# Banks of PSUM dealt out anew in two phases of attention heads, and the last output written in two pieces

## The chip, the cores and the metric

The kernel runs on one core of a Trainium2 chip, as one program. The metric is the device time of one execution in microseconds (us), lower is better. TensorE (PE in the profile) multiplies matrices into PSUM, which has eight banks of 128 partitions x 512 float32 values; VectorE (DVE) and ScalarE (ACT) read the banks; SyncE (SP) issues the transfers (DMA) from memory.

## The reference

Two layers of a decoder for 256 tokens of 1024 values. Each layer is attention, then a SwiGLU feed-forward part, both behind an RMS norm whose shift, scale and gate come from a vector c by a matrix (the modulation):

```python
mod = jax.nn.silu(c) @ ada_w[i] + ada_b[i]
sh_a, sc_a, g_a, sh_f, sc_f, g_f = jnp.split(mod[:, None, :], 6, axis=-1)
h = rms_norm(x, attn_norm[i]) * (1.0 + sc_a) + sh_a
y = sparse_mixer(h, ...) if i % 2 == 0 else diff_mixer(h, ...)
x = x + g_a * y
h = rms_norm(x, ffn_norm[i]) * (1.0 + sc_f) + sh_f
x = x + g_f * swiglu(h, ffn_w_gate[i], ffn_w_up[i], ffn_w_down[i])
```

Layer 0 has eight MoBA heads and eight NSA heads and one output projection over both. Layer 1 is differential attention: eight heads, each of two soft-max maps, `a = p0 - lam * p1`, then `a @ v`, a norm of each head's output, and the output projection.

## The kernel before

Every large matrix arrives in row tiles of 128 x 1024 (512 KB) in a ring of five buffers, `raw`. ScalarE rounds a tile to `hi` (L188), VectorE takes the rest as `lo` (L189), and three matmuls (hi, lo, hi) make a product of nearly full precision (`mm3`). Activations lie transposed as pairs of such parts in `bigT`. All matmuls outside transposes go through `mm` (L114 to L116), so the profile shows them as L116.

`banks(acc, sc, tr, ot)` says which banks the next phase takes for what: `SC` for scores, `TR` for transposes, `OT` for the heads' outputs. `bank(*SC)` deals them out in turn. In the second phase of heads of both layers `SC` is 0, 1, 2, `TR` is 4, 5, `OT` is 6, 7, and bank 3 is handed to the modulation. In the phase ahead of it in both layers `TR` is 6, 7, and transposes that began there still use them.

A head pair goes through these steps. `softmax_maps` (L878) takes a bank for each of two maps, multiplies q by k (TensorE), then for each half of the tokens VectorE adds the mask and finds the maximum (L892), and ScalarE takes the exponential (L894) into tiles `s`, of which there are four. `transpose_map` (L908) transposes a map by three matmuls with the identity (L911) into a bank of `TR`, and ScalarE copies it to `pT` (L913). `av` (L916) multiplies `pT` with the values into a bank of `OT`, in two steps by key block. In layer 0 `split` then makes `bigT` of the bank. In layer 1 `diff_heads` (L1227) combines two maps into one ahead of the transposes (L1253 to L1257), copies the output to `od`, and `finish` (L1230) norms it, multiplies it (L1236), transposes it (L1238) into a bank of `TR` and splits it.

Beside the heads runs `ada_pe` (L323), for columns j = 4 and then 3 of the modulation: VectorE clears a bank (L326), then eight raw tiles come (L329), and each takes four matmuls of one output row, `raw,cs` in the profile. ScalarE copies the sums out (L318), two transposes (L320) turn them into columns, and VectorE adds the bias (L355).

`weave` calls the generators of heads and of modulation in turn, and `late` chains them. That is the order in which the code records; the order on each engine is set by the framework's scheduler from dependencies and its own estimates. Each engine, and SP's queue of transfers, runs its list strictly in order. Behind the heads comes `out_proj` (L533) into banks 0 to 3, with eight tiles of weights through the same `raw` ring, then `res_norm` (L442), whose transposes are L407.

At the end of layer 1's feed-forward part (`ffn`, L674 to L680) the last six blocks of the down projection are kept back: for each half of the tokens (t) and of the columns (f) 18 matmuls of 512 columns close one bank, and `res_norm` multiplies that bank by the gate (L452), adds it to `xs` (L455) and sends the 256 KB out (L457).

## Time and profile before

| | us |
|---|---|
| median of three runs (lowest, highest) | 751.43 (750.35, 752.98) |
| the profiled execution | 752.87 |
| its span | 750.8 |
| PE busy | 706.4 (94%) |
| DVE busy | 504.5 (67%) |
| ACT busy | 414.6 (55%) |
| share of the 16 DMA engines taken by the queue of transfers | 61.9% |

Busy time of PE is modelled and overlaps, so 94% is not TensorE at its peak. The chain of work that ended last says what kept the end back; the timeline lists the instructions in order of time, with the idle time ahead of one in brackets and what ended it; windows give busy time, granted clock of TensorE (PEclk, 1.00 is 2.4 GHz and 0.50 is 1.2 GHz) and DMA share of a stretch. In the timeline one matmul leaves one or two records, so the four matmuls on one raw tile show as x8. `kTm,qTm` and `kTn,qT` are scores, `ident,s` transposes of maps, `pT,...` and `pcT,vblk` products with values, `hi,bigT` and `lo,bigT` out_proj.

### The profile page before, as it was taken

The numbers are of one execution on the slowest core, as the hardware profiler recorded it, in microseconds if no ns is written. First come the engines' busy times: TensorE is split into PE (matmuls) and PEld (weight loads), VectorE is DVE, ScalarE is ACT, GpSimd is POOL, SyncE is SP. The second block draws the span as 40 slices with busy tenths as digits, with TensorE's granted clock in tenths as the row PEclk, the third lists the DMA queues.
The fourth block names the chain that finished last, engine by engine and source line by source line (L and its number), as shares of the span: only waits on it lengthen the run. The fifth ranks groups of instructions, "written<-read, shape, count | busy, mean of one in ns | idle before, by whom it ended". The sixth has DMA issues, their size and how long they took to land.

```text
span 750.8 us, 10789 instructions
## 1 busy us (share of the span) xinstructions
PE 706.4 (94%) x3822; PEld 540.6 (72%) x3822; DVE 504.5 (67%) x1078; ACT 414.6 (55%) x813; POOL 40.8 (5%) x131
## 2 busy tenths in 40 slices
PE   5799899799989999999999999997989999999997
PEld 1368567445668878888887787763667888888885
DVE  3558565666587789788855765846777796655632
ACT  3465734688466456545544665566557465555530
POOL 5004102000000000000000021110000000000000
PEclk9999999799999999999999999899899999999999
DMA  9938286067538899998851564008937886566501
GB/s 321 379 127 313 76 296 246 1 234 276 192 91 274 284 339 338 314 305 299 280 193 60 196 223 141 29 18 304 345 113 257 309 292 212 172 196 192 179 20 57
DMA packets 86525, 159.41 MB, mean 212 GB/s; under 512 B 6199, under 2 KB 48316, under 8 KB 86472
## 3 DMA queue, kind: packets, MB, share of 16 engines
q1 hardware_dynamic: 85992, 158.72, 61.9%
q8 instruction: 30, 0.49, 0.3%
q14 instruction: 23, 0.19, 0.1%
q0 software_dynamic: 480, 0.01, 0.0%
HBM read 157.66 MB, written 1.05 MB: 211 GB/s over the span
## 4 chain that ended last, share of the span: by engine, by line
PE 77%; DMA 8%; DVE 6%; ACT 5%; issue 3%; SPq 1%; DVEq 0%; ACTq 0%
PE bank L116 73%; PE bank L911 2%; DMA araw<-in_ada_w_dram 2%; DMA bias<-in_ada_w_dram 2%; DMA raw<-in_ada_w_dram 1%; DMA raw<-in_sp_w_in_dram 1%; DVE lo L189 1%; DMA xs<-in_x_dram 1%; DMA raw<-in_ffn_w_gate_dram 1%; PE bank L711 1%; ACT hi L188 1%; DVE ada_acc L282 1%; PE bank L407 1%; ACT bigT L188 1%; DVE bigT L189 1%
## 5 line engine op out<-in xcount | busy, mean ns | idle before, releaser
L189 DVE TENSOR_TENSOR lo<-raw,hi 128x1024 fp32r<-128x1024 f32 x131 | 156.6, 1205 | 54.2 <-ACT hi L188 53.6
L188 ACT ACTIVATE hi<-raw 128x1024 fp32r<-128x1024 f32 x131 | 135.2, 1043 | 69.9 <-PE bank L116 43.3
L116 PE MATMUL bank<-hi,bigT 128*128 128x512 f32 (+1 forms) x472 | 154.0, 397 | 5.2 <-ACT bigT L188 4.4
L116 PE MATMUL bank<-bigT,hi 128*128 128x512 f32 (+1 forms) x400 | 130.8, 379 | 0.0
L116 PEld LDWEIGHTS bank<-hi,bigT 128*128 128x128 f32 x472 | 89.2, 192 | 26.0 <-ACT bigT L188 5.3
L116 PE MATMUL bank<-bigT,lo 128*128 128x256 f32 x368 | 98.5, 281 | 0.0
L116 PE MATMUL bank<-lo,bigT 128*128 128x512 f32 (+1 forms) x236 | 93.8, 398 | 0.5 <-DVE lo L189 0.4
L116 PEld LDWEIGHTS bank<-bigT,hi 128*128 128x128 f32 x400 | 71.7, 189 | 12.8 <-DVE lo L189 0.4
L282 DVE SCALAR_TENSOR_TENSOR ada_acc<-araw,cs,ada_acc 128x1024 f32<-128x1024 f32 x46 | 58.8, 1278 | 20.1 <-DMA araw<-in_ada_w_dram 20.1
L116 PEld LDWEIGHTS bank<-bigT,lo 128*128 128x128 f32 x368 | 69.5, 189 | 3.8 <-issue 0.2
L116 PEld LDWEIGHTS bank<-lo,bigT 128*128 128x128 f32 x236 | 45.3, 192 | 13.4 <-DVE lo L189 3.9
L892 DVE CUSTOM_DVE_ANT_0 s<-bank,maskc,nrs 128x128 f32<-128x128 f32 (+1 forms) x80 | 29.9, 412 | 32.0 <-PE bank L116 15.5
L620 ACT ACTIVATE w2k<-bank 128x256 f32<-128x256 f32 x64 | 23.9, 379 | 34.0 <-PE bank L116 34.0
L894 ACT ACTIVATE s<-s,mx 128x128 f32<-128x128 f32 (+1 forms) x80 | 35.7, 448 | 10.5 <-DVE mx L892 10.3
L621 DVE TENSOR_TENSOR w2k<-bank,w2k 128x256 f32<-128x256 f32 x64 | 26.5, 417 | 10.0 <-ACT w2k L620 10.0
L116 PE MATMUL bank<-bigT,nkv 128*128 128x256 f32 (+1 forms) x176 | 31.5, 322 | 0.0
L189 DVE TENSOR_TENSOR tok<-raw,tok 128x1024 fp32r<-128x1024 f32 x19 | 23.2, 1220 | 9.2 <-ACT tok L188 9.1
L188 ACT ACTIVATE nkv<-raw 128x1024 fp32r<-128x1024 f32 x19 | 20.1, 1057 | 16.1 <-PE bank L116 8.1
L189 DVE TENSOR_TENSOR nkv<-raw,nkv 128x1024 fp32r<-128x1024 f32 x19 | 23.2, 1222 | 7.7 <-ACT nkv L188 7.6
L188 ACT ACTIVATE tok<-raw 128x1024 fp32r<-128x1024 f32 x19 | 20.1, 1058 | 13.7 <-PE bank L116 9.5
L116 PEld LDWEIGHTS bank<-bigT,nkv 128*128 128x128 f32 x176 | 25.5, 188 | 2.8
L394 ACT ACTIVATE xn<-xs 128x512 f32<-128x512 f32 x16 | 10.1, 630 | 30.1 <-DVE xs L455 24.3
(342 smaller groups left out, 1257.7 us busy)
## 6 DMA issues: line engine op xcount, KB each, us to landing
araw<-in_ada_w_dram SPq DMA_DIRECT2D x50, 512.0 KB, 5.3
raw<-in_ffn_w_gate_dram SPq DMA_DIRECT2D x44, 512.0 KB, 5.1
raw<-in_ffn_w_up_dram SPq DMA_DIRECT2D x44, 512.0 KB, 4.9
raw<-in_ffn_w_down_dram SPq DMA_DIRECT2D x44, 512.0 KB, 5.2
raw<-in_ada_w_dram SPq DMA_DIRECT2D x32, 512.0 KB, 5.1
raw<-in_diff_w_in_dram SPq DMA_DIRECT2D x24, 512.0 KB, 4.5
raw<-in_sp_w_in_dram SPq DMA_DIRECT2D x20, 512.0 KB, 6.0
raw<-in_nsa_cmp_w_dram SPq DMA_DIRECT2D x8, 512.0 KB, 5.1
```

The lines of the kernel that those rows point to most:

```text
L116: ins = T.matmul(o, lhsT=lhsT, rhs=rhs, start=start, stop=stop).ins
L188: i1 = A.activation(out=hi, in_=src, func=AF.Copy)
L189: i2 = V.tensor_tensor(out=lo, in0=src, in1=hi.bitcast(F32), op=ALU.subtract)
L282: ins = V.scalar_tensor_tensor(out=acc, in0=raw, scalar=cs[:, k:k + 1], in1=acc, op0=ALU.mult, op1=ALU.add)
L394: return A.activation(out=junk[:, fs], in_=xs[:, t, fs], func=AF.Square, accum_out=ss[:, f:f + 1])
L407: q = T.transpose(out=b[:, k * P:(k + 1) * P], in_=xn[:, f * 512 + k * P:f * 512 + (k + 1) * P], identity=ident)
L620: A.activation(out=s[:, f * S:(f + 1) * S], in_=bs[f][:, S:512], func=AF.Copy)
L621: V.tensor_tensor(out=s[:, f * S:(f + 1) * S], in0=bs[f][:, 0:S], in1=s[:, f * S:(f + 1) * S], op=ALU.add)
L711: T.transpose(out=b[:, k * P:(k + 1) * P], in_=src[:, k * P:(k + 1) * P], identity=ident)
L892: V.tensor_tensor_reduce(out=s[:, o:o + n], in0=b[:, o:o + n], in1=maskc[:, S - n:S], scale=nr(t), scalar=3e38, op0=ALU.add, op1=ALU.min, ...
L894: A.activation(out=s[:, o:o + n], in_=s[:, o:o + n], func=AF.Exp, scale=-1.0, bias=mx[:, t:t + 1], accum_out=sm[:, t:t + 1])
L911: T.transpose(out=b[:, k * P:(k + 1) * P], in_=s[:, k * P:(k + 1) * P], identity=ident)
```

## The change

In both phases `SC` gets a fourth bank, 3; `OT` keeps bank 6 alone; the modulation's bank is 7 instead of 3. At the end, for the last half of tokens and of columns, the 18 matmuls become 2 x 18 of 256 columns each, and multiplication, addition and transfer go in two pieces of 256 columns. Both pieces lie in the same bank, and only the last of the 36 matmuls has `stop` set. Lines behind the additions move by 7 (from L451 on) and by 17 (from L678 on).

```diff
--- before.py
+++ after.py
@@ -448,6 +448,13 @@
         marks = []
         for f in range(2):
             fs = slice(f * 512, (f + 1) * 512)
+            if last and t and f:
+                for e in (512, 768):
+                    es = slice(e, e + 256)
+                    V.tensor_tensor(out=xn[:, es], in0=bs[t][f][:, e - 512:e - 256], in1=g[:, es], op=ALU.mult)
+                    V.tensor_tensor(out=xs[:, t, es], in0=xs[:, t, es], in1=xn[:, es], op=ALU.add)
+                    dma(out[0, t * P:(t + 1) * P, es], xs[:, t, es])
+                return
             y = xn[:, fs]
             m = V.tensor_tensor(out=y, in0=bs[t][f], in1=g[:, fs], op=ALU.mult)
             if t and not last:
@@ -674,6 +681,16 @@
             keep = chain[:]
             chain[:] = tail
             for fs in ((0,), (1,)):
+                if nxt[2] is None and t and fs[0]:
+                    for e in (0, 256):
+                        for k in ks:
+                            ah, al = acts[k // 2]
+                            cc = slice((k % 2) * S + t * P, (k % 2) * S + (t + 1) * P)
+                            hi, lo = us[k - ks[0]]
+                            c = slice(512 + e, 768 + e)
+                            mm3(BS[t][1][:, e:e + 256], ah[:, cc], al[:, cc], hi[:, 0, c], lo[:, 0, c], False,
+                                e > 0 and k == ks[-1])
+                    continue
                 for k in ks:
                     down_mm(t, k, us[k - ks[0]], fs)
             tail[:] = chain
@@ -1297,12 +1314,12 @@
     nh = nsa_heads(*on)
     weave((late(np_, first(nh, 6)), 22), (moba_proj(hts), 20), (ada(0, 2, pin=True), 9))
     hts = new_hts()
-    banks([], [0, 1, 2], [4, 5], [6, 7])
+    banks([], [0, 1, 2, 3], [4, 5], [6])
     settle()
     plan((), R5)
     ordr = [4, 5, 6, 7, 0, 1, 2, 3]
     pre = [row_unit(sp_w_out[0], ordr[m]) for m in range(1)]
-    weave((late(nh, moba_heads(*om)), 22), (late(*[ada_pe(0, j, bank_tiles[3]) for j in (4, 3)]), 14))
+    weave((late(nh, moba_heads(*om)), 22), (late(*[ada_pe(0, j, bank_tiles[7]) for j in (4, 3)]), 14))
     plan(R5[1:] + (('qT', 'kTn'), 'tok4'), R5)
     banks([], [], FGU, [])
     drain(out_proj([om, on], sp_w_out[0], ordr, rows[(0, 2)], (0, 3, hts), pre))
@@ -1323,8 +1340,8 @@
     ob_ = pair()
     hts = new_hts()
     plan(R5 + (('qT', 'kTn'), 'tok4'), R5)
-    banks([], [0, 1, 2], [4, 5], [6, 7])
-    weave((diff_heads(1, st, *ob_), 12), (late(*[ada_pe(1, j, bank_tiles[3]) for j in (4, 3)]), 14))
+    banks([], [0, 1, 2, 3], [4, 5], [6])
+    weave((diff_heads(1, st, *ob_), 12), (late(*[ada_pe(1, j, bank_tiles[7]) for j in (4, 3)]), 14))
     banks([], [], FGU, [])
     drain(out_proj([oa, ob_], diff_w_out[0], range(8), rows[(1, 2)], (1, 3, hts)))
     plan(*FFN_PLAN)
```

How this moves instructions is shown at three places. In the names `bank_67` is bank 0, `bank_70` bank 3, `bank_71` to `bank_74` banks 4 to 7.

Layer 0, TensorE, near the end of the heads. Before (`pT,vm` are products with values, `ident,s` transposes of maps, `hi`, `lo`, `qT`, `kTn`, `tok` out_proj's weights):

```order
L116 MATMUL bank_74<-pT_1794,vm_784 64x256 [waits Activation_49]
L116 MATMUL bank_74<-pT_1786,vm_784 64x128
L116 MATMUL bank_74<-pT_1794,vm_784 64x128
L911 MATMUL bank_72<-ident,s_1814 128x128 x3
L320 MATMUL bank_71<-ident,w2k_1844 128x128 [waits Activation_49]
L320 MATMUL bank_71<-ident,w2k_1844 128x128
L116 MATMUL bank_73<-pT_1834,vm_784 64x256
L116 MATMUL bank_67<-tok_1979,bigT_771 128x512 [waits Activation_49]
L116 MATMUL bank_67<-tok_1980,bigT_771 128x512 [waits DVE_49]
L116 MATMUL bank_67<-tok_1979,bigT_771 128x512 [waits DVE_49]
L116 MATMUL bank_73<-pT_1842,vm_784 64x256 [waits Activation_49]
L116 MATMUL bank_73<-pT_1834,vm_784 64x128
```

After, at the same maps:

```order
L928 MATMUL bank_71<-ident,s_1812 128x128 [waits Activation_49]
L928 MATMUL bank_71<-ident,s_1812 128x128 [waits DVE_49]
L928 MATMUL bank_71<-ident,s_1812 128x128
L928 MATMUL bank_72<-ident,s_1814 128x128 [waits Activation_49]
L928 MATMUL bank_72<-ident,s_1814 128x128 [waits DVE_49]
L928 MATMUL bank_72<-ident,s_1814 128x128
L116 MATMUL bank_67<-qT_1973,bigT_771 128x512 [waits Activation_49]
L116 MATMUL bank_67<-kTn_1974,bigT_771 128x512
L116 MATMUL bank_73<-pT_1786,vm_784 64x256 [waits DVE_49]
L116 MATMUL bank_73<-pT_1794,vm_784 64x256
L116 MATMUL bank_73<-pT_1786,vm_784 64x128
L116 MATMUL bank_73<-pT_1794,vm_784 64x128
```

The three transposes of one map and of its partner stand together, and the four matmuls with the values of one pair stand in one run instead of two.

Layer 1, VectorE, the clearing of the modulation's bank. Before (`L892` are the score reductions of a map, `s` and `mx` their results):

```order
L892 ISA s_4761,mx_4771<-bank_68,maskc,nrs_4223 128x256
L892 ISA mx_4771 128x1
L892 ISA s_4763,mx_4774<-bank_69,maskc,nrs_4223 128x256
L892 ISA mx_4774 128x1
L892 ISA s_4811,mx_4815<-bank_67,maskc,nrs_4223 128x128 [waits PE_49,Activation_49]
L892 ISA mx_4815 128x1
L326 MEMSET bank_70 128x256 [waits Activation_49]
L892 ISA s_4813,mx_4818<-bank_68,maskc,nrs_4223 128x128 [waits PE_49]
L892 ISA mx_4818 128x1
L892 ISA s_4811,mx_4821<-bank_67,maskc,nrs_4223 128x256 [waits DVE_49]
```

After (`L909` are the same reductions, `L1274` the combination of two maps, `L1253` the multiplication of od):

```order
L1253 SCALAR_TENSOR_TENSOR od_4422<-od_4422,rs_y_4700,gout 128x128 [waits DVE_49]
L1253 SCALAR_TENSOR_TENSOR od_4422<-od_4422,rs_y_4700,gout 128x128 x3
L1274 SCALAR_TENSOR_TENSOR s_4863<-s_4865,sm_4866,s_4863 128x256
L909 ISA s_4961,mx_4966<-bank_70,maskc,nrs_4223 128x128 [waits PE_49]
L909 ISA mx_4966 128x1
L909 ISA s_4959,mx_4969<-bank_69,maskc,nrs_4223 128x256
L909 ISA mx_4969 128x1
L909 ISA s_4961,mx_4972<-bank_70,maskc,nrs_4223 128x256
L909 ISA mx_4972 128x1
L189 TENSOR_TENSOR bigT_4218<-bank_74,bigT_4218 128x256 [waits Activation_49]
L189 TENSOR_TENSOR bigT_4218<-bank_73,bigT_4218 128x256 [waits Activation_49]
L326 MEMSET bank_74 128x256 [waits DVE_49]
```

The clearing moved from behind the fifth reduction of the phase to behind all sixteen, behind od's multiplications and the two splits of the banks 7 and 6.

The same place on TensorE, where the first matmuls on raw tiles wait for it. Before:

```order
L116 MATMUL bank_69<-kTm_4220,qTm_4219 128x128 [waits DVE_49]
L116 MATMUL bank_69<-kTm_4220,qTm_4219 128x256
L116 MATMUL bank_70<-raw_4749,cs 1x256 [waits DMAHW4_49,DVE_49]
L116 MATMUL bank_70<-raw_4749,cs 1x256 x3
L116 MATMUL bank_70<-raw_4777,cs 1x256 [waits DMAHW5_49]
L116 MATMUL bank_70<-raw_4777,cs 1x256 x3
```

After (`L1255` are od's transposes, `nkv,pT` products with values):

```order
L928 MATMUL bank_71<-ident,s_4863 128x128 [waits DVE_49,Activation_49]
L1255 MATMUL bank_74<-ident,od_4422 128x128 [waits DVE_49] x2
L1255 MATMUL bank_73<-ident,od_4422 128x128 [waits DVE_49] x2
L928 MATMUL bank_71<-ident,s_4863 128x128 [waits DVE_49]
L928 MATMUL bank_71<-ident,s_4863 128x128
L116 MATMUL bank_73<-nkv_4221,pT_4791 128x128 [waits DVE_49]
L116 MATMUL bank_73<-nkv_4221,pT_4791 128x128
L116 MATMUL bank_73<-nkv_4222,pT_4791 128x128
L116 MATMUL bank_74<-raw_4749,cs 1x256 [waits DMAHW4_49,DVE_49]
L116 MATMUL bank_74<-raw_4749,cs 1x256 x3
```

The matmuls on raw tiles moved from behind the scores of the third map to behind the transposes of three maps, od's transposes and a product with values.

The tail on VectorE. Before:

```order
L455 TENSOR_TENSOR xs<-xs,xn_6821 128x512 [waits DVE_49]
L452 TENSOR_TENSOR xn_6865<-bank_69,mod_6743 128x512 [waits PE_49]
L455 TENSOR_TENSOR xs<-xs,xn_6865 128x512 [waits DVE_49]
L452 TENSOR_TENSOR xn_6865<-bank_70,mod_6743 128x512 [waits PE_49]
L455 TENSOR_TENSOR xs<-xs,xn_6865 128x512 [waits DVE_49]
```

After:

```order
L459 TENSOR_TENSOR xn_6883<-bank_69,mod_6743 128x512 [waits PE_49]
L462 TENSOR_TENSOR xs<-xs,xn_6883 128x512 [waits DVE_49]
L454 TENSOR_TENSOR xn_6883<-bank_70,mod_6743 128x256 [waits PE_49]
L454 TENSOR_TENSOR xn_6883<-bank_70,mod_6743 128x256
L455 TENSOR_TENSOR xs<-xs,xn_6883 128x256 [waits DVE_49] x2
```

One multiplication and one addition became two of each; the second multiplication waits for nothing of its own.

## Rows read from the trace of the kernel before

**Rows 1.** The page's chain that ended last: share of the span by engine
```profile
PE 77%; DMA 8%; DVE 6%; ACT 5%; issue 3%; SPq 1%; DVEq 0%; ACTq 0%
```

**Rows 2.** Windows: us, then PE, PEld, DVE, ACT, POOL busy (count); PEclk; DMA share; GB/s
```profile
180.00:190.00 10.00, 10.00 (x53) 6.89 (x47) 8.75 (x20) 10.00 (x24) 0.00 (x0) 1.00 0.82 290
...
512.00:516.00 4.00, 3.35 (x23) 2.50 (x21) 2.88 (x13) 3.79 (x19) 0.00 (x0) 1.00 1.02 409
...
524.00:528.00 4.00, 2.21 (x19) 0.71 (x19) 2.48 (x13) 0.43 (x2) 0.00 (x0) 0.70 1.01 389
528.00:532.00 4.00, 3.39 (x10) 2.37 (x9) 3.08 (x4) 3.82 (x6) 0.00 (x0) 0.50 1.01 396
532.00:536.00 4.00, 4.00 (x19) 3.23 (x18) 3.35 (x5) 2.77 (x4) 0.00 (x0) 0.95 0.91 315
```

**Rows 3.** Timeline, layer 0, PE: start us, busy us, engine, line, out<-in, records
```profile
146.74 0.88 PE L116 MATMUL bank<-pT,nkv 128*64 128x256 f32 x8
147.55 0.55 PE L911 MATMUL bank<-ident,s 128*128 128x128 f32 x3
...
157.05 0.65 PE L116 MATMUL bank<-pT,nkv 128*64 128x256 f32 x2
157.63 0.55 PE L911 MATMUL bank<-ident,s 128*128 128x128 f32 x3
158.11 0.61 PE L116 MATMUL bank<-raw,cs 128*1 128x256 f32 x8
158.65 0.86 PE L116 MATMUL bank<-pT,nkv 128*64 128x256 f32 x6
159.45 0.55 PE L911 MATMUL bank<-ident,s 128*128 128x128 f32 x3
...
164.63 0.93 PE L116 MATMUL bank<-kTm,qTm 64*128 64x128 f32 x8
165.49 0.65 PE L116 MATMUL bank<-pT,nkv 128*64 128x256 f32 x2
...
166.55 1.04 PE L116 MATMUL bank<-raw,cs 128*1 128x256 f32 x16
167.52 0.86 PE L116 MATMUL bank<-pT,nkv 128*64 128x256 f32 x6
```

**Rows 4.** Timeline, layer 0, PE: first run, the one wait, and the stretch's end
```profile
149.46 0.65 PE L116 MATMUL bank<-pT,nkv 128*64 128x256 f32 x4
...
198.19 0.86 PE L116 MATMUL bank<-pT,vm 128*64 128x256 f32 x6 [0.59 <-ACT pT L913]
...
210.84 1.04 PE L407 MATMUL bank<-ident,xn 128*128 128x128 f32 x8
```

**Rows 5.** Timeline, layer 1, PE: first modulation, first refilled raw tile, start of out_proj
```profile
503.81 2.34 PE L116 MATMUL bank<-raw,cs 128*1 128x256 f32 x40
...
508.18 0.61 PE L116 MATMUL bank<-raw,cs 128*1 128x256 f32 x8 [0.68 <-DMA raw<-in_ada_w_dram]
...
528.95 2.07 PE L116 MATMUL bank<-hi,bigT 128*128 128x512 f32 x4 [0.61 <-ACT hi L188]
```

**Rows 6.** Timeline, layer 1, DVE: the memset of the modulation's bank, the second bigT split
```profile
503.49 0.27 DVE L326 MEMSET bank<- 128x256 f32 x1
...
513.39 0.42 DVE L189 TENSOR_TENSOR bigT<-bank,bigT 128x256 fp32r<-128x256 f32 x1
```

**Rows 7.** Chain of waits, layer 1: start us, us, what ended it
```profile
519.77 6.65 DMA raw<-in_ada_w_dram
...
527.95 0.95 ACT hi L188
```

**Rows 8.** Timeline, tail: matmuls of 256 columns on PE, the last multiplication on DVE
```profile
716.05 1.58 PE L116 MATMUL bank<-bigT,tok 128*128 128x256 f32 x12
717.47 1.59 PE L116 MATMUL bank<-bigT,nkv 128*128 128x256 f32 x12
...
746.09 0.69 DVE L452 TENSOR_TENSOR xn<-bank,mod 128x512 f32<-128x512 f32 x1 [2.77 <-PE bank L116]
```

## The prediction

> **What bounds the kernel now.** I read the chain of work that ended last first: 77% of the span is TensorE at work, 8% waits for DMA [rows 1]. So time can come only from TensorE being kept from its work, or from work that TensorE does badly. The three stretches that the change touches differ in this. In the second phase of heads of layer 0, with its out_proj (149.46 to 210.84 us [rows 4]), the windows show TensorE busy all the time, and no wait but one of 0.59 us [rows 2, 4]. What is lost there is seen only in the timeline: inside a run of matmuls of one kind starts follow at 0.05 to 0.11 us, but from the last start of a run to the first of another kind 0.2 to 0.3 us pass, and 64 such runs stand between 149.46 and the transposes of the next norm at 210.84. I read a run's price from its first start to the next run's: 0.58 us for a product with the values of two records, 0.80 for one of six, 0.81 for one of eight, 0.48 for three transposes, 0.54 for the modulation's matmuls on one raw tile, 0.97 on two, 0.86 for a pair's scores [rows 3]. In layer 1 the same phase is bound elsewhere: TensorE is busy 2.21 of 4 us in 524:528, while the DMA engines are full [rows 2], and the longest links of the chain are waits for modulation weights [rows 7]. In the tail TensorE ends, then VectorE multiplies and adds 512 columns, then the last DMA goes out [rows 8].
>
> **Layer 0.** The work stays, its order changes: with a fourth bank the scores of a pair stand further ahead of their use, transposes come six together instead of three, and the two halves of a product with the values, which had transposes or modulation between them, stand in one run in five places. I priced every run of both orders with the prices above. Products with the values: 17 runs become 12; five times 0.58 + 0.80 becomes one of 0.81, so 13.06 goes to 10.23 us, -2.83. Modulation: 12 runs to 9, and each run saved is worth 2 x 0.54 - 0.97 = 0.11 or, where it had been cut inside a tile, up to 0.5; together -0.74. Transposes of maps: 15 runs to 12, -0.34. Scores: 6 to 8 runs, since four are now cut to a half or quarter, +0.89. The few runs of out_proj and of the modulation's own transposes: -0.28. Sum -3.30, from 60.1 to 56.8 us of priced work, against 61.4 in the trace [rows 4]. What is above the price is waits, 0.59 us of it in [rows 4]; with maps ready earlier that one should go. But new ones can come: four banks of scores are also out_proj's accumulators, so its first matmuls into the banks read last now stand behind VectorE's reading of them, and the last heads' output has its split behind a single bank. I bound these by nothing and by the 0.59 of [rows 4] at two places, 1.2. The one bank for heads' outputs adds no other wait: the next product follows over a microsecond behind the split. So layer 0 gives between -4.1 and -2.1; I take the middle, **-3.1**. No later stage holds this back: 210.84 and everything after it is released by events, not by a clock.
>
> **Layer 1.** Here the same rule of banks moves the modulation. Its bank 7 was a transposing bank of the phase ahead, and od's transposes of the first pair still go there. So the memset of bank 7 on VectorE, at 503.49 in the trace, now stands behind the soft-max of all four maps, od's multiplications and the two bigT splits; before it stood five scores reductions into the phase. All that stands ahead of it was done in the trace when the second bigT split ended, at 513.39 + 0.42 [rows 6]. Less its own memset, and with the four transposes in one group, I put the new memset at 513.3 to 513.6 and the first matmul on a raw tile at 513.9, between 513.0 and 515.0, against 503.81 [rows 5]. What queues behind that wait on TensorE: products with values of the later maps, and with each of the 16 raw tiles the release of one of five raw buffers, thus SP's issue of the next transfer, the last eight of which are the weights of out_proj. The price runs through DMA: from the first modulation matmul to the landing of the first refilled tile 508.18 - 503.81 = 4.37 us [rows 5]; then 512 KB at 409 GB/s is 1.28 us each [rows 2]. The first out_proj tile is the twelfth: 4.37 + 11 x 1.28 = 18.45; the hi split takes 0.95 [rows 7], with the step to TensorE 1.05. So out_proj starts 19.5 us behind the first modulation matmul, at 533.4 instead of 528.95 [rows 5]: +4.5. The delay of 10.1 us is not all paid, because before, the stream stood still between the two modulations (the chain's 6.65 us [rows 7]), which the new order doesn't. Against this stands a price of the clock: out_proj begins at half clock, 0.50 in 528:532 and 0.95 in 532:536 [rows 2], behind a stretch in which TensorE waited; the excess is about half of 3.5 us, 1.7. By this estimate TensorE idles earlier and longer, from 505 to 514, and meets out_proj with sparse modulation matmuls, so the excess is the same 1.7 or, with one more such stretch, 3.4; I take it as 0.5 more, nearer to the row: **+5.0**, between +3.0 (first matmul at 513.0, no half clock left) and +7.3 (515.0 and one more such 1.7).
>
> **Tail.** The 18 matmuls of 512 columns become 36 of 256. Twelve of 256 take 717.47 - 716.05 = 1.42 us in the trace [rows 8], 0.118 each, so 36 take 4.26 against 18 x 0.233 = 4.19, +0.07. The two pieces are in one bank and only the last matmul signals, so VectorE begins where it began: four operations of 256 columns, 0.42 us with 0.34 between starts (the bigT split in [rows 6]), against two of 0.69 [rows 8]: 1.44 to 1.68 against 1.40. The last DMA is half as large. Net between -0.4 and +0.4, taken **+0.1**. If the first piece were free to start while the second's 2.1 us of matmuls run, it would save 0.7; the order has no such wait.
>
> **A rule weighed.** In layer 0 the trace shows no wait for a bank, 10.00 of 10 us busy with ScalarE as full in 180:190 [rows 2]; what I count as gain is only the change of kind. The Trainium skill (TensorE: Matmul & The Clock Gate, section HAM oscillation) tells of a kernel in which double-buffered PSUM gave no further gain once TensorE was kept fed; by it the fourth bank is worth nothing here, layer 0 is 0 and the sum +5.1. The rows give -3.1, because the order changes with the banks.
>
> **The rivals.**
> - *The late modulation is hidden* (faster). If VectorE reaches the memset early, or out_proj's first weights don't bind, layer 1 costs 0 to 2.5. It decides at 528.95 - 19.5 = 509.4: a first modulation matmul before that costs nothing. For it: the pause in the stream goes. Against it: the memset's place on VectorE, 10 us of work further back. Own time 752.87 - 3.1 + 0.1 to + 2.6, so 748.4 to 750.9.
> - *The fourth bank buys nothing* (slower): ScalarE, full in 180:190 [rows 2], sets the pace of layer 0, and the drains that go are replaced by waits for its pT copies. It decides where ScalarE's idle time in that phase ends. Layer 0 is 0, the sum +5.1: 756.5. This is also what the page's sentence would give.
> - *Half clock through out_proj* (slower): TensorE's long idle stretch in layer 1 keeps the granted clock at 0.50 for a second stretch as long as that in [rows 2]: +1.7, 755.1. It decides where the clock rises, before or after the first raw tile of out_proj is used up. The Trainium skill (same page, Why this matters for your kernels) warns of idle gaps between bursts; the 0.70 in 524:528 agrees.
> - *The tail overlaps after all*: -0.7, inside the forecast's range.
>
> **How the numbers follow.** Sum -3.1 + 5.0 + 0.1 = +2.0. The profiled execution took 752.87 us (span 750.8), so it would take 754.9; it is 1.44 above the median of the three runs, 751.43, so against that 753.4. Its own range is 751.5 to 755.3. What can be told from no change is 0.3%, 2.25 us: 749.2 to 753.7. Chances: forecast 0.48 (same 0.30, slower 0.18); modulation hidden 0.19 (faster 0.11, same 0.08); fourth bank buys nothing 0.13 (slower); half clock 0.10 (slower); several small things otherwise 0.10 (same 0.06, slower 0.04). Together faster 0.11, same 0.44, slower 0.45. The range leaves out the lower half of the hidden case and the top of the slow ones: 749.2 to 756.8.
>
> **What would show it.** Layer 0: the transposes of the next norm at 207.7 instead of 210.84, 54 runs, TensorE still without gaps. Layer 1, all 3.1 earlier: first modulation matmul near 510.8, behind a memset that ends then; DMA nearly idle until 511.5, then full without a pause; out_proj at 530.3, 19.5 us behind the first modulation matmul instead of 25.1; half clock at its start. Tail: four VectorE rows of 256 columns in a row behind the last matmul. I am wrong if the memset runs before 509 in the old count, if layer 0 ends less than 2 us earlier, or if out_proj in layer 1 starts at once at full clock.

## The result, and the profile after

The changed kernel is slower: 758.65 us median (757.61 to 758.85, four runs), against 750.89 (748.90 to 752.98) for the kernel before on the same chip; the ratio on record is 1.0121, 95% interval 1.0094 to 1.0148 (the two medians alone give 1.0103). The prediction had 753.4 and a range up to 756.8, so it had the direction and not the size: 2.0 us were forecast, 7.8 came. The profiled execution took 758.58 us (span 756.9) against 752.87 (750.8).

The page's chain that ended last now reads (share of the span by engine):

```profile
PE 69%; DMA 12%; DVE 8%; ACT 6%; issue 2%; SPq 1%; DVEq 0%; ACTq 0%
```

Against [rows 1] TensorE's share fell from 77% to 69%, and those of DMA, VectorE and ScalarE rose from 8, 6 and 5%: TensorE is kept from its work for longer. To see where, follow TensorE's timeline of after (start us, busy us, engine, line, out<-in, records, idle before and its releaser) through the landmarks of the prediction: the start of layer 0's phase, the end of its out_proj, the first scores of layer 1's two phases of heads, the first modulation matmul, out_proj, the next norm:

```profile
125.97 1.97 PE L116 MATMUL bank<-kcT,qT 128*128 128x32 f32 x16
...
205.72 1.03 PE L407 MATMUL bank<-ident,xn 128*128 128x128 f32 x8
...
459.71 0.93 PE L116 MATMUL bank<-kTn,qT 64*128 64x128 f32 x8
...
498.13 0.93 PE L116 MATMUL bank<-kTm,qTm 64*128 64x128 f32 x8
...
513.36 3.59 PE L116 MATMUL bank<-raw,cs 128*1 128x256 f32 x32
...
535.76 1.20 PE L116 MATMUL bank<-hi,bigT 128*128 128x512 f32 x4 [0.80 <-ACT hi L188]
...
558.89 1.03 PE L407 MATMUL bank<-ident,xn 128*128 128x128 f32 x8
```

The same landmarks of before, where they are not in [rows 4, 5]:

```profile
128.30 1.97 PE L116 MATMUL bank<-kcT,qT 128*128 128x32 f32 x16
...
465.14 0.93 PE L116 MATMUL bank<-kTn,qT 64*128 64x128 f32 x8
...
500.29 0.93 PE L116 MATMUL bank<-kTm,qTm 64*128 64x128 f32 x8
...
553.15 1.03 PE L407 MATMUL bank<-ident,xn 128*128 128x128 f32 x8
```

Subtracting neighbours gives the account of the two profiled executions, in us (the tail's row goes from the last norm to VectorE's last multiplication, 746.09 in [rows 8] and 752.31 after):

| stretch | before | after | difference | predicted |
|---|---|---|---|---|
| start to layer 0's phase | 128.30 | 125.97 | -2.33 | 0 |
| layer 0: phase and out_proj | 82.54 | 79.75 | -2.79 | -3.1 |
| to layer 1's heads | 254.30 | 253.99 | -0.31 | 0 |
| layer 1, first phase of heads | 35.15 | 38.42 | **+3.27** | 0 |
| second phase, to the first modulation matmul | 3.52 | 15.23 | +11.71 | +10.1 |
| from there to out_proj | 25.14 | 22.40 | -2.74 | -5.6 |
| out_proj | 24.20 | 23.13 | -1.07 | +0.5 |
| rest, to the last multiplication | 192.94 | 193.42 | +0.48 | +0.1 |

The first row is chance: the fourteen profiled executions come in two kinds that part within the first 42 us, by about 4 us, and the one of before was of the late kind (this landmark stands at 124.2 to 126.6 eleven times, at 128.3 to 128.7 three times). So below, single terms are judged by stretches of the traces, whole kernels by their ratio.

The expensive rows are in layer 1. VectorE, second phase (the same columns):

```profile
508.46 1.13 DVE L1253 SCALAR_TENSOR_TENSOR od<-od,rs_y,gout 128x128 f32<-128x128 f32 x4
...
510.98 0.75 DVE L189 TENSOR_TENSOR bigT<-bank,bigT 128x256 fp32r<-128x256 f32 x2
511.78 0.27 DVE L326 MEMSET bank<- 128x256 f32 x1
```

TensorE beside it, ahead of the first modulation matmul at 513.36, and the waits of the chain (start us, us, what) that follow up to out_proj:

```profile
511.79 1.65 PE L116 MATMUL bank<-nkv,pT 128*128 128x128 f32 x6 [1.05 <-DVE bigT L189]
```

```profile
519.20 7.83 DMA raw<-in_ada_w_dram
...
527.75 5.62 DMA raw<-in_ada_w_dram
```

Windows of after (us, then PE, PEld, DVE, ACT, POOL busy; PEclk; DMA share; GB/s):

```profile
508.00:512.00 4.00, 2.37 (x9) 1.42 (x9) 3.95 (x18) 3.08 (x11) 0.00 (x0) 0.50 0.00 0
512.00:516.00 4.00, 4.00 (x34) 2.09 (x38) 1.25 (x6) 1.48 (x8) 0.00 (x0) 0.50 0.13 24
516.00:520.00 4.00, 4.00 (x40) 2.17 (x32) 0.50 (x3) 1.20 (x6) 0.00 (x0) 0.80 0.94 320
520.00:524.00 4.00, 2.11 (x27) 0.52 (x26) 1.96 (x12) 1.58 (x7) 0.00 (x0) 1.00 1.01 380
...
532.00:536.00 4.00, 1.90 (x19) 0.65 (x20) 1.18 (x4) 1.97 (x5) 0.00 (x0) 1.00 0.99 355
```

VectorE is full while TensorE stands at half clock and no DMA moves at all; then, from 520 on, the DMA engines are full, at less than the 409 GB/s of [rows 2]. This is the predicted picture, only larger. What the prediction does not have is the stretch before it. TensorE in layer 1's first phase, where no line was changed; before:

```profile
471.95 1.60 PE L911 MATMUL bank<-ident,s 128*128 128x128 f32 x6
473.43 1.65 PE L116 MATMUL bank<-vm,pT 128*128 128x128 f32 x6
475.01 1.66 PE L116 MATMUL bank<-kTn,qT 64*128 64x128 f32 x8
476.60 1.50 PE L116 MATMUL bank<-vm,pT 128*128 128x128 f32 x6
```

After:

```profile
467.00 1.08 PE L928 MATMUL bank<-ident,s 128*128 128x128 f32 x3 [0.31 <-DVE s L1274]
468.31 2.05 PE L116 MATMUL bank<-kTn,qT 64*128 64x128 f32 x8 [0.22 <-DVE mx L909]
470.29 1.65 PE L116 MATMUL bank<-vm,pT 128*128 128x128 f32 x6
473.59 1.65 PE L116 MATMUL bank<-vm,pT 128*128 128x128 f32 x6 [1.66 <-ACT od L1284]
```

The scores of the fourth pair of maps (the last `kTn,qT` rows) and the first product with values (`vm,pT`) have changed places. ScalarE then has the fourth pair's exponentials (L911) to do ahead of copying that product's output to `od` (L1284), and the second product waits 1.66 us for the copy. ScalarE in after:

```profile
472.45 0.49 ACT L911 ACTIVATE s<-s,mx 128x256 f32<-128x256 f32 x1
...
472.94 0.60 ACT L1284 ACTIVATE od<-bank,sm 128x128 f32<-128x128 f32 x2
```

### The profile page after: what moved, and what is told of

Same layout as the page of the kernel before. It is cut to its first block, busy times and chain, and to the rows that moved or that the text cites. A ratio compares the mean times of both kernels' runs of the same rounds, so it can differ in the third digit from the quotient of the medians.

```text
span 756.9 us, 10831 instructions
## 1 busy us (share of the span) xinstructions
PE 704.2 (93%) x3840; PEld 542.8 (72%) x3840; DVE 505.9 (67%) x1080; ACT 415.2 (55%) x813; POOL 40.5 (5%) x131
## 3 DMA queue, kind: packets, MB, share of 16 engines
HBM read 157.66 MB, written 1.05 MB: 210 GB/s over the span
## 4 chain that ended last, share of the span: by engine, by line
PE 69%; DMA 12%; DVE 8%; ACT 6%; issue 2%; SPq 1%; DVEq 0%; ACTq 0%
PE bank L116 66%; DMA araw<-in_ada_w_dram 3%; DMA raw<-in_ada_w_dram 3%; DMA raw<-in_sp_w_in_dram 2%; DMA bias<-in_ada_w_dram 1%; DMA raw<-in_ffn_w_gate_dram 1%; ACT s L911 1%; PE bank L928 1%; DVE lo L189 1%; DMA xs<-in_x_dram 1%; DVE s L909 1%; ACT hi L188 1%; DMA raw<-in_diff_w_out_dram 1%; DVE bigT L189 1%; PE bank L728 1%
## 5 line engine op out<-in xcount | busy, mean ns | idle before, releaser
L116 PE MATMUL bank<-hi,bigT 128*128 128x512 f32 (+1 forms) x472 | 151.7, 392 | 7.1 <-ACT bigT L188 4.4
L909 DVE CUSTOM_DVE_ANT_0 s<-bank,maskc,nrs 128x128 f32<-128x128 f32 (+1 forms) x80 | 29.9, 413 | 34.0 <-PE bank L116 16.2
L911 ACT ACTIVATE s<-s,mx 128x128 f32<-128x128 f32 (+1 forms) x80 | 35.6, 448 | 11.1 <-DVE mx L909 10.4
L189 DVE TENSOR_TENSOR tok<-raw,tok 128x1024 fp32r<-128x1024 f32 x19 | 23.2, 1221 | 10.1 <-ACT tok L188 10.1
L394 ACT ACTIVATE xn<-xs 128x512 f32<-128x512 f32 x16 | 10.1, 629 | 33.2 <-DVE xs L462 26.9
L188 ACT ACTIVATE tok<-raw 128x1024 fp32r<-128x1024 f32 x19 | 20.1, 1057 | 13.6 <-PE bank L116 10.4
```

The costliest lines, as they stand in the source:

```text
L116: ins = T.matmul(o, lhsT=lhsT, rhs=rhs, start=start, stop=stop).ins
L188: i1 = A.activation(out=hi, in_=src, func=AF.Copy)
L189: i2 = V.tensor_tensor(out=lo, in0=src, in1=hi.bitcast(F32), op=ALU.subtract)
L394: return A.activation(out=junk[:, fs], in_=xs[:, t, fs], func=AF.Square, accum_out=ss[:, f:f + 1])
L909: V.tensor_tensor_reduce(out=s[:, o:o + n], in0=b[:, o:o + n], in1=maskc[:, S - n:S], scale=nr(t), scalar=3e38, op0=ALU.add, op1=ALU.min, ...
L911: A.activation(out=s[:, o:o + n], in_=s[:, o:o + n], func=AF.Exp, scale=-1.0, bias=mx[:, t:t + 1], accum_out=sm[:, t:t + 1])
```

## Experiments

Ratios are against the kernel before on the same chip, with 95% intervals; they are the ratios on record, not the quotients of the two medians. Of an edit only the lines that matter are shown, and `...` stands for lines left out; a line put in without the one that it replaces replaces the same line as in l0 or l1.

### The three parts alone

**l0**, the banks of layer 0 alone:

```
-    banks([], [0, 1, 2], [4, 5], [6, 7])
+    banks([], [0, 1, 2, 3], [4, 5], [6])
...
-    weave((late(nh, moba_heads(*om)), 22), (late(*[ada_pe(0, j, bank_tiles[3]) for j in (4, 3)]), 14))
+    weave((late(nh, moba_heads(*om)), 22), (late(*[ada_pe(0, j, bank_tiles[7]) for j in (4, 3)]), 14))
```

> Kernel before with the new banks in layer 0 alone. Theory A (two effects that cancel): the second phase of heads of layer 0 with its out_proj ends about 2.8 us earlier counted from 130 us, but layer 1's first phase of heads, which has no changed line, loses about 2.9 us between 465 and 478 us as in the changed kernel, because the banks 0, 1, 2 are dealt out in turn by one counter for layer 0's scores and layer 1's accumulators, and it now stands at another bank. Time within 1 us of before. Rival B (the loss at 470 us came from layer 1's own new banks, or is chance): no loss there, 2.8 us faster, 748.1.

750.89 against 749.48 us; 1.0030 [1.0003, 1.0057]. In the trace the stretch from the first matmul on `kcT` to the next norm takes 78.97 us instead of 82.54, but layer 1's first phase takes 39.51 instead of 35.15: layer 0's gain (part of the 3.57 us is the clock's, as the point on layer 0 below works out) is lost 250 us further on, in code of which no line differs. The loss is larger than expected, and the kernel is a little slower than before, not within 1 us of it.

**l1**, the same edit in layer 1 alone:

```
-    banks([], [0, 1, 2], [4, 5], [6, 7])
-    weave((diff_heads(1, st, *ob_), 12), (late(*[ada_pe(1, j, bank_tiles[3]) for j in (4, 3)]), 14))
+    banks([], [0, 1, 2, 3], [4, 5], [6])
+    weave((diff_heads(1, st, *ob_), 12), (late(*[ada_pe(1, j, bank_tiles[7]) for j in (4, 3)]), 14))
```

> Kernel before with the new banks in layer 1 alone. Theory A: first matmul on a modulation tile 15 us behind the phase's first scores instead of 3.5, out_proj 37.6 us behind them instead of 28.7, out_proj itself 1.1 us shorter since the clock is up again, no loss at 465 to 478: 8.3 us slower, about 759. Rival B: the loss at 470 us shows here: 11 us slower, about 762. Rival C (most of the changed kernel's loss was chance of DMA): 5 us slower, 756.

759.4 us; 1.0140 [1.0098, 1.0181]. The first phase keeps its 35.14 us; the second reaches out_proj after 38.66 instead of 28.66 us. So layer 1's banks alone cost about 10 us, twice what the prediction put down for them.

**tail**, the output in two pieces alone (the first two pieces of the change's diff).

> Kernel before with the tail in two pieces alone. Theory A: VectorE starts behind the last of 36 matmuls, four operations one behind another, nothing overlaps; the last transfer is half as large: -0.3 to +0.3 us, no difference that can be measured. Rival D (the pieces overlap or the smaller transfer pays): 0.7 us faster.

747.55 us; 0.9980 [0.9954, 1.0007], no difference that can be told. The rows of after show why: the second multiplication follows the first at once, and both stand behind TensorE's last matmul, as the one multiplication does in [rows 8]:

```profile
752.31 0.76 DVE L454 TENSOR_TENSOR xn<-bank,mod 128x256 f32<-128x256 f32 x2 [2.79 <-PE bank L116]
752.98 0.75 DVE L455 TENSOR_TENSOR xs<-xs,xn 128x256 f32<-128x256 f32 x2
```

### Which of the two bank edits delays layer 1's second phase

**l1_ada7**: in layer 1 the modulation in bank 7 and one bank for outputs, but three banks for scores.

```
+    banks([], [0, 1, 2], [4, 5], [6])
+    weave((diff_heads(1, st, *ob_), 12), (late(*[ada_pe(1, j, bank_tiles[7]) for j in (4, 3)]), 14))
```

> Kernel before with, in layer 1 alone, the modulation in bank 7 and heads' outputs in bank 6, and three banks of scores as before. Theory A (bank 7 is what costs, since od's transposes of the phase ahead still use it, so its clearing stands behind them): first matmul on a modulation tile 12 us or more behind the first scores instead of 3.5, 7 to 10 us slower, 757 to 760. Rival F (the fourth bank of scores costs, by putting all score reductions ahead on VectorE): modulation starts early, time within 2 us of before.

**l1_b3**: the modulation stays in bank 3; bank 7 becomes the fourth bank for scores.

```
+    banks([], [0, 1, 2, 7], [4, 5], [6])
```

> Kernel before with, in layer 1 alone, four banks of scores (0, 1, 2, 7), outputs in bank 6 and the modulation left in bank 3. Theory A: clearing early, first modulation matmul within 3.5 us of the first scores, out_proj no later than 28.7 us behind them, time within 2 us of before. Rival F: 5 us slower or more.

l1_ada7: 756.57 us; 1.0098 [1.0063, 1.0133]. Without any fourth bank the first modulation matmul is 14.49 us behind the first scores and out_proj 37.23, as in the changed kernel (15.23 and 37.63): bank 7 for the modulation is enough for the loss (the one bank for outputs, which frees bank 7, isn't the cause: l1_two below has it, too, and is fast).

l1_b3: 756.75 us; 1.0102 [1.0053, 1.0151]. Here the first clearing is early, the first modulation matmul 3.56 us behind the scores, and still out_proj comes 35.09 us behind them: the expectation, 28.7 us at most and no loss, fell. The windows and the chain of l1_b3 name a second way to the same loss:

```profile
508.00:512.00 4.00, 2.42 (x17) 1.47 (x17) 3.76 (x22) 4.00 (x19) 0.00 (x0) 1.00 1.02 415
512.00:516.00 4.00, 2.77 (x12) 2.37 (x13) 2.87 (x15) 3.65 (x16) 0.00 (x0) 0.61 0.12 47
516.00:520.00 4.00, 2.71 (x17) 1.67 (x20) 3.34 (x18) 1.86 (x8) 0.00 (x0) 0.50 0.00 0
```

```profile
517.89 1.14 DVE od L1236 x4
...
519.08 0.27 DVE bank L326
```

The clearing for the second modulation (j=3) stands behind the other pair's `od` on VectorE, at 519.08, 23.0 us behind the scores, and the stream is empty for 8 us. Both modulations share one bank, so the second can begin only when the first is copied out and the bank is cleared again.

**l1_two**: that dependence taken away, too. Three banks for scores, one for outputs, and for each of the two modulations a bank of its own; the late-free bank 7 goes to the second.

```
+    banks([], [0, 1, 2], [4, 5], [6])
+    weave((diff_heads(1, st, *ob_), 12), (late(*[ada_pe(1, j, bank_tiles[n]) for j, n in ((4, 3), (3, 7))]), 14))
```

> Kernel before with, in layer 1 alone, heads' outputs in bank 6 and the bank so freed, 7, given to the second half of the modulation (j = 3), while the first half (j = 4) stays in bank 3. Theory A (what bounds the second phase of heads in layer 1 is when the two clearings of modulation banks come, since the weights stream behind them): the first clearing stays early, the second no longer waits for ScalarE's copy of the first half, the pause in the stream of weights goes, out_proj starts 23 to 25 us behind the first scores instead of 28.7, and the norm behind it follows 3 to 5 us earlier: 744 to 746, 0.4 to 0.7% faster. Rival H (the stream's length or the heads themselves bound out_proj's start, not the clearings): within 1 us of before in that phase, no difference in the time.

746.61 against 749.71 us; 0.9957 [0.9937, 0.9978], faster than the kernel before. Bank 7 is cleared at 509.89 here, later than an early start would want, but by then it is only the second modulation that needs it, and TensorE waits 0.80 us for the clearing:

```profile
510.22 0.61 PE L116 MATMUL bank<-raw,cs 128*1 128x256 f32 x8 [0.80 <-DVE bank L326]
```

Out_proj starts 24.99 us behind the scores instead of 28.66 [rows 5], and no half clock is left from the first scores to the next norm.

### Where layer 0's gain goes

**l0_ot1**: in layer 0 one bank for outputs, with three for scores and the modulation in bank 3.

```
+    banks([], [0, 1, 2], [4, 5], [6])
```

> Kernel before with, in layer 0 alone, heads' outputs in bank 6 only, three banks of scores and the modulation in bank 3 as before. Its order has 12 runs of products with values as the changed kernel has, but 12 of modulation and 16 of transposes. Theory A (the price of runs): the phase from 149.5 to the next norm's transposes is 1.0 us shorter than before, 2.3 longer than in l0. Rival G (the fourth bank is what brings the gain): no gain at all. Whole time within 0.3% of before either way; the trace decides.

746.76 us; 0.9965 [0.9938, 0.9992]. Layer 0's stretch takes 81.12 us, with 6.8 us of it at half clock; two kernels without the new banks and with as much half clock (l1, l1_two) take 82.55 and 82.66. So the single bank for outputs, whose two products have to stand in one run, is worth about 1.5 us by this one trace. Layer 1's first phase stays at 35.52.

**l0_turn**: l0, with the counter that deals out banks 0, 1, 2 set on by one behind layer 0's heads, so that later phases get the banks in the same turn as before.

```
+    bank_at[(0, 1, 2)] = bank_at.get((0, 1, 2), 0) + 1
```

> As l0, and the counter that deals out banks 0, 1, 2 is advanced by one behind layer 0's heads, so that layer 1 begins with the same bank as before. Theory A: layer 0's 2.8 us stay and the 2.9 us in layer 1's first phase are not lost: about 748, some 0.37% faster than before. Rival B: the same time as l0.

749.96 us; 1.0013 [0.9990, 1.0035]. Layer 1's first phase is still 39.24 us, so the expectation fell: the turn of the banks is not the cause.

**l0_hold**: l0_turn, and the fourth pair's scores in layer 1's first phase are held behind the first product with values, an order and no wait.

```
-    def softmax_maps(qks, nrs):
+    def softmax_maps(qks, nrs, behind=None):
...
-                    mm(b[:, 0:P], lhsT=qh[:, 0:P], rhs=kh[:, 0:P], start=True, stop=True)
+                    q = mm(b[:, 0:P], lhsT=qh[:, 0:P], rhs=kh[:, 0:P], start=True, stop=True)
+                    if behind:
+                        after(q, behind)
...
+                                  avs[hh - 3] if part == 0 and hh >= 3 else None)
...
+                avs.append(mm(ob[:, P:S], lhsT=aT[:, S:S + P], rhs=vh(1), start=False, stop=True))
```

> As l0_turn, and in layer 1's first phase of heads the scores of the fourth map are kept behind the first product with values, as they stand in the kernel before. Theory A2 (the 4 us that l0, l0_turn and the changed kernel lose between 465 and 480 us come from that one exchange: eight more exponentials stand ahead of od's copy on ScalarE, TensorE waits for it, and its clock falls for longer): that loss goes, layer 0's 3.4 us stay: 746, 0.4% faster than before, and 3 to 4 us faster than l0_turn. Rival E (the clock's fall at that place is chance): the loss stays in its trace or differs from run to run, time as l0_turn, 750.

748.30 against 748.57 us; 0.9985 [0.9954, 1.0016]. The first phase is back at 35.78 us. TensorE's timeline of l0_hold has the old order:

```profile
465.94 1.84 PE L914 MATMUL bank<-ident,s 128*128 128x128 f32 x6
468.55 1.65 PE L116 MATMUL bank<-vm,pT 128*128 128x128 f32 x6 [0.78 <-ACT pT L916]
470.13 1.65 PE L116 MATMUL bank<-kTn,qT 64*128 64x128 f32 x8
471.71 1.24 PE L116 MATMUL bank<-vm,pT 128*128 128x128 f32 x6
```

So the exchange, with the half clock that came with it (13.6 us in l0_turn's phase, 6.8 here), is what cost 3.5 us. About 0.6 us stay against the kernel before, where the first product has no wait of 0.78 us for ScalarE. The time of the whole kernel, expected at 746 us, moved by less than the intervals can tell from l0_turn; the stretch is the evidence. Why the scheduler made the exchange was not found.

### Together

**after_hold**: the changed kernel with that order held, and the counter set on as in l0_turn.

> The changed kernel, but the scores of the fourth map in layer 1's first phase of heads stand behind the first product with values again, as they stand before the change (and the counter of the three banks goes one further after layer 0's heads, as in the other run with this order). Theory: the 3.3 us that the changed kernel loses between the first scores on kTn and the first on kTm (38.42 us against 35.15) come from the order of these two alone, so this stretch takes 35.5 to 36 us and the time is 3 us (2.4 to 3.6) below the changed kernel's, near 755.5 us; the late clearing stays, out_proj's first matmul stays 37 to 38 us behind the first scores on kTm. Rival: the stretch is slow for the banks and not for the order; then it stays at 38 us and the time at 758.6 us.

757.77 us; 1.0105 [1.0070, 1.0140], against 1.0121 for the changed kernel: no gain that can be told. The expectation fell, and the trace says how. The first phase does take 36.57 us instead of 38.42, but the scheduler has moved the second phase as well; TensorE in after_hold:

```profile
498.94 3.47 PE L116 MATMUL bank<-kTm,qTm 64*128 64x128 f32 x16 [0.53 <-DVE mx L912]
...
504.49 1.09 PE L931 MATMUL bank<-ident,s 128*128 128x128 f32 x3 [1.25 <-DVE s L1279]
507.24 1.26 PE L1258 MATMUL bank<-ident,od 128*128 128x128 f32 x4 [1.66 <-DVE od L1256]
```

All scores now stand ahead of the first transposes, the combinations of all four pairs stand ahead of the clearing (of three in after), TensorE is at half clock from 500 on, and the first modulation matmul is 16.40 us behind the scores (15.23 in the changed kernel), out_proj 39.57 (37.63). What the first phase gained, 1.85 us, the second lost, 1.94. In the changed kernel the two losses could not be taken apart by one edit.

**all_two**: l0_hold and l1_two in one kernel. **all_tail**: the same with the tail in two pieces.

> l0_hold and l1_two together: new banks in layer 0, the order of layer 1's first phase held, two banks for the modulation in layer 1. Theory A: the gains add, layer 0 about 2.5 us, layer 1 3 to 5 us: 741 to 744, 0.7 to 1% faster than before. Rival H: as l0_hold alone, 748.

> The fastest kernel so far (in layer 0 four banks for scores, one for heads' outputs; in layer 1 a bank for each of the two modulations; the scores of layer 1's first phase in the old order) with the output's tail in two pieces added. Theory: the tail's first piece overlaps nothing, so its two pieces cost or give 0.2 us at most and the time is that kernel's, 745.5 to 746.5 us, ratio 0.995. Rival: with the earlier end of the phase the tail's first write overlaps the last sums, and the time is 744.5 us or less.

all_two: 745.70 against 749.71 us; 0.9954 [0.9935, 0.9973]. all_tail: 745.14 against 750.71; 0.9938 [0.9911, 0.9965]. They can't be told from each other; both beat the kernel before and the changed one. The expectation for all_two, 741 to 744 us with the gains added up, fell: its ratio is that of l1_two alone (0.9957), and no kernel here shows layer 0's gain in its whole time. What is left of that gain, about 2.0 us less the 0.5 that the held order doesn't give back, is 0.2% and less than the intervals can tell. The tail's rows in all_tail are those of after, 2.79 us of idle and then four operations.

## Why the prediction was wrong, point by point

Two steps failed: the sum put layer 1's first phase of heads at nothing, and it lost 3.27 us; and it put the start of out_proj in layer 1 at +4.5, and +8.97 came.

- **Layer 0, -3.1 (between -4.1 and -2.1): the right direction, about 2.0 in size.** The profiled pair gives -2.79, but not at one clock. Windows of before, then of after (the same columns as above), near the start of the stretch:

```profile
140.00:150.00 10.00, 9.23 (x55) 5.89 (x52) 6.92 (x27) 6.82 (x24) 0.00 (x0) 0.66 0.00 0
```

```profile
140.00:150.00 10.00, 9.31 (x72) 5.26 (x73) 7.29 (x29) 6.95 (x26) 0.00 (x0) 1.00 0.21 69
```

  Before spent 10.2 us of the stretch at half clock, after 3.4. The fourteen traces can be compared at equal half clock: with 3.4 us of it the stretch takes 79.5 us on average in five kernels with these banks and 81.6 in two without, with 10.2 us 80.7 in two and 82.6 in two. So the gain is 1.9 to 2.1 us, at the near end of the range, and some 0.8 of the -2.79 was luck with the clock, not the edit. New waits are larger than the 1.2 allowed, 1.7 in all: 0.53 and 0.78 us at the two places that the prediction named, VectorE's reading of a scores bank and the last split, and 0.40 for a raw tile. The rival that the fourth bank buys nothing, and with it the sentence weighed from the Trainium skill (TensorE: Matmul & The Clock Gate, HAM oscillation), is not refuted: the edit as a whole made a phase shorter in which TensorE had been fed before, but l0_ot1 has about 1.5 of the 2.0 us without a fourth bank, and the fourth bank was not run alone.
- **"No later stage holds this back": the step that failed first.** It put the first phase of layer 1 at 0. True of the events, but the order of the list is not an event. The scheduler orders the whole program, and a change in layer 0 exchanged two groups in layer 1's first phase, +3.27 us. l0, l0_turn and l0_hold show it. The difference of the two orders has that row; the prediction looked at the phases whose lines changed, alone.
- **Layer 1, the mechanism: right.** The memset of bank 7 stands behind od's multiplications and both splits, the modulation starts late, the stream of weights starts late, out_proj waits. l1_ada7 shows that the bank of the modulation alone does it. One reading was off without harm to the sum: the 6.65 us of [rows 7] are a wait for one landing, and the stream itself stood still for 2.7 us (from 516.71 to 519.40).
- **Layer 1, the size: +4.5 to the start of out_proj, measured +8.97** (37.63 less 28.66). Two terms were mis-sized. *First modulation matmul*, +10.1 predicted, +11.71 measured: the memset ends 13.92 us behind the first scores, where the prediction had the matmul start at 13.6, so 0.3 of it. The other 1.3 is the product with values that stands between, 1.57 us from its start to the next at half clock, and waits for the same splits as the memset. It stands in the pieces of order shown ahead of the prediction, and was not priced. *From there to out_proj*, 19.5 predicted, 22.40 measured. By the times at which the transfers landed, the first refilled tile comes 4.42 us behind (4.37 predicted), and the last step takes 1.13 (1.05). But the eleven steps between take 16.85 us instead of 14.1. The rate was not wrong: eight of the eleven take 1.25 to 1.29 us, as priced. Three take 2.50, 1.67 and 2.51. TensorE's rows for the late tiles, and the steady ones behind them:

```profile
520.32 0.61 PE L116 MATMUL bank<-raw,cs 128*1 128x256 f32 x8 [0.32 <-DMA raw<-in_ada_w_dram]
...
522.00 0.61 PE L116 MATMUL bank<-raw,cs 128*1 128x256 f32 x8 [1.06 <-DMA raw<-in_ada_w_dram]
...
527.08 0.61 PE L116 MATMUL bank<-raw,cs 128*1 128x256 f32 x8 [0.40 <-DMA raw<-in_ada_w_dram]
528.35 0.61 PE L116 MATMUL bank<-raw,cs 128*1 128x256 f32 x8 [0.67 <-DMA raw<-in_ada_w_dram]
...
533.41 0.61 PE L116 MATMUL bank<-raw,cs 128*1 128x256 f32 x8 [0.66 <-DMA raw<-in_ada_w_dram]
```

  For the last of the three the trace has a candidate. Each transfer signals its landing in 16 parts. Up to the tile that landed at 524.52 the last part came at most 0.22 us behind the last but one; from the next, at 527.03, it came about 1.25 us behind, for five tiles. Between them, from 524.98 for 1.0 us, the DMA engines carried one packet of 16 KB of instructions (DMA view of after in 524:528: queue and kind, packets, MB, share of the 16 engines):

```profile
q8 instruction: 1, 0.02, 1.6%
```

  In the kernel before such a packet came at 518.35, while the stream stood still. In each of the seven kernels whose stream does not stop, one of the two landings behind it comes 1.83 to 2.51 us after the one ahead. That fits, but no run moved the packet, so it is not shown. What delays the first two steps was not found; they are late in the same way in l1 (2.51 and 1.72), and in l1_ada7 and after_hold the first takes 3.4.
- **Half clock in out_proj, +0.5: didn't come**, -1.07. PEclk is 1.00 from 520 on, so out_proj started at full clock, one of the prediction's own signs of being wrong. TensorE stood at half clock earlier, in the wait, at 0.50 in 508:516. after_hold, whose clock does fall again, shows that this was no certainty: there PEclk is 0.50 in 532:536. The 1.6 us between +0.5 and -1.07 made the total look better than the account.
- **Tail, +0.1: right.** -0.2 from the last multiplication to the end, and no overlap. (The +0.48 in the table's last row is no part of it: the next norm's stretch takes 10.41 us, 3.4 of them at half clock, and 9.55 in before and the other traces.)
- **The sum.** Predicted -3.1 + 5.0 + 0.1 = +2.0; without the start of the execution, which is chance, the traces give -2.8 - 0.3 + 3.3 + 9.0 - 1.1 + 0.3 = +8.4, and the medians +7.8. Missing were 3.3 in a first phase that was thought untouched and 4.5 in the second, and 1.6 in out_proj stood against them.

The share of the clock in the first phase is seen from kernels with one order there: at half clock for 6.8 us of the phase it takes 35.64 and 35.78 (all_two, l0_hold), for 10.2 us it takes 36.54 and 36.57 (all_tail, after_hold). So 3.4 us more at half clock cost 0.85, and of after's +3.27 (10.2 us at half clock) about 1.9 are the exchange itself; the rest, about 0.5, stays in the kernels with the order held.

## What to carry to other kernels

Where a scheduler orders the program, read the difference of the orders over the whole program, above all in phases that wait, and not only where a line changed. A bank that holds a sum over streamed tiles should be one that is free when the stream could start; if two such sums share a bank, the clearing between them stops the stream, and a second bank, even a late one, is worth more than a fourth for scores. For a stream of many tiles forecast single late tiles beside the rate: here eight steps of eleven came at the rate, and three cost 2.8 us. Price each instruction that stands between the wait and the work it releases. And compare a stretch of two traces only at equal time at half clock.

## What the runs showed of the hardware

- The granted clock differs between executions of one kernel, and the time mostly with it: the twelve of all_tail range from 743.38 us at a mean of 0.991 to 750.63 at 0.974.
- What half clock costs: in layer 0's stretch 6.8 us more of it took 1.2 us in kernels with the new banks (79.5 to 80.7) and 1.1 without (81.6 to 82.6); in layer 1's first phase 3.4 us more took 0.85.
- Most tiles of the stream of 512 KB tiles land 1.24 to 1.30 us behind the one ahead, before the change and after. Nearly all that the stream loses, it loses in a few late steps, two to five among the eleven in the kernels where it doesn't stop, of 1.4 to 3.4 us. The GB/s of a window don't show this: in 528:536 of after they are 354 and 355 with the engines full (share 1.00 and 0.99), and the tiles still land 1.25 to 1.28 us apart.
- Most single packets of the stream took 0.16 us; some took 1.0 to 1.6, in before and in after.
- Windows of all_tail around layer 1's first phase; TensorE's clock falls after a window in which it was busy 1.51 of 4 us and stays at 0.50 through two in which it was busy 3.52 and 3.34:

```profile
464.00:468.00 4.00, 1.51 (x10) 0.92 (x8) 2.55 (x15) 3.60 (x13) 0.00 (x0) 0.93 0.00 0
468.00:472.00 4.00, 3.52 (x14) 2.34 (x14) 3.63 (x19) 2.20 (x9) 0.00 (x0) 0.50 0.01 4
472.00:476.00 4.00, 3.34 (x15) 2.47 (x16) 1.87 (x10) 3.62 (x14) 0.00 (x0) 0.50 0.00 0
```
